# Row halves of the TensorE array for the second rotary product of the attention scores

## The chip, the cores and the metric

The kernel runs on one core of a Trainium2 chip. The metric is the device time of one execution in microseconds (us); the kernel before was run three times, and its median is the number to compare with. The engines are TensorE (PE, with its weight loads shown as PEld), VectorE (DVE), ScalarE (ACT), GpSimd (POOL) and SyncE (SP), which here issues most of the DMA transfers. TensorE works from SBUF into PSUM, which has banks of 512 f32 values in each of 128 partitions.

## What is computed

One layer of an encoder for two sequences of 1024 tokens: a low-rank attention with four heads and a Fourier mixing side by side, an output projection, and a feed-forward part. Of this the attention matters here. Each query and key has a part without position (128 dims, here absorbed into the 128 latent dims of the keys) and a rotary part of 64 dims; the rotary key is shared by the four heads:

```python
q = (rmsnorm(q_lat, g_q_lat) @ w_uq).reshape(b, s, MLA_HEADS, QK_DIM)
q_nope, q_pe = q[..., :NOPE_DIM], q[..., NOPE_DIM:]
q_pe = apply_rope(q_pe, cos[:, None, :], sin[:, None, :])
k_pe = apply_rope(k_pe, cos, sin)
sc = (jnp.einsum('bqhd,bkhd->bhqk', qn_b, k_nope)
      + jnp.einsum('bqhr,bkr->bhqk', qp_b, k_pe)).astype(jnp.float32) * scale
p = jax.nn.softmax(sc, axis=-1).astype(v.dtype)
return jnp.einsum('bhqk,bkhd->bqhd', p, v)
```

## The kernel before

All arithmetic on TensorE that must hold f32 precision is done on split numbers: a value x is written as a high part in f32r (copied by ACT in `split`, line 63) and a low part x minus high (DVE, line 64). A product of two split matrices is three matmuls, high times high, high times low, low times high (`mm3`, lines 79 to 81); low times low is left out.

The kernel goes through stages one after the other: input projections and the first Fourier step, the Fourier step over the tokens with its output, the attention, and the feed-forward part, which is by far the longest and uses a Strassen-like scheme of seven products. Stages share the SBUF: pools of tiles are opened and closed, and a tile that lies over an older one waits until that one's readers are done.

In the attention stage a loop of 64 steps goes over the two sequences s, four blocks b of 256 queries, four heads h, and two halves u of 128 queries. A step issues:
- `scores` (line 1025): ten matmuls of 128 rows by 512 columns into two PSUM banks, five for each bank g of 512 keys. Three of them are the latent part (lines 1033 to 1035, stationary `qa`, the absorbed query, high and low), two the rotary part (lines 1036 and 1037, stationary `qp`). Behind them come the maximum over the keys (DVE, line 1042), the exponential (ACT, line 1047) and the division (DVE, line 1049).
- `flip_p` for the step before: eight transposes of the probabilities on TensorE (line 1061) into PSUM tiles of the tag t (two buffers), each four split by ACT and DVE.
- `values` for a head that is finished (24 matmuls through `mm3`), and a part of the output projection, of the norm and of its transposes for an earlier block (`out_step`).
- for the next block of queries, at the fourth and fifth steps of eight, `rope_q`, which computes the rotary queries, and at the sixth and seventh steps `rope_flip`, which transposes them; and `absorb_q` for the next head.

How the rotary part lies: `rope_q` puts the high part of the 64 rotary dims into columns 0 to 63 of a tile and the low part into columns 64 to 127. `rope_flip` transposes this for four heads (line 720), so in `qp` the rows 0 to 63 are the high part and 64 to 127 the low part of the query; ACT copies it out of PSUM at line 722. The keys stand in `lat[0][:, 1]` (high) and `lat[1][:, 1]` (low), where the 64 rotary dims are held twice, in rows 0 to 63 and again in 64 to 127. One matmul of 128 rows so gives the sum of query high and query low times a key part: line 1036 with the key's high part, line 1037 with its low part.

The order of the instructions on each engine is not just the order of the program: the framework plans it at build time with a cost for every instruction, takes what is ready by its plan in the order of the program, and puts the semaphores. So matmuls of `values` can stand between the transposes of `flip_p`. Each engine then works through its queue in order.

Elsewhere the kernel already uses parts of the array: the modulation vectors at lines 214 and 907 are products with 32 columns of the array each, four next to each other, and line 303 uses two of 64 columns. They hold all 128 rows and are in plain f32, without a split. The transposes of line 374 and the products of lines 79 to 81 that stand around them use the whole array.

Of the kernel before, what the change touches and what calls it, by code (L numbers as in the profile page):

```python
# [13 lines left out]
F32R = mybir.dt.float32r  # L14
# [7 lines left out]
P = 128  # L22
# [3 lines left out]
HEADS = 4  # L26
# [27 lines left out]
def hybrid_encoder_kernel(ctx: ExitStack, tc: tile.TileContext, a: dict):  # L54
    nc = tc.nc
# [3 lines left out]
    def rd(t):  # L59
        return t.bitcast(F32)  # L60
# [5 lines left out]
    def first(early, late):  # L66

        tc.add_manual_dep(late, early.name, mybir.DependencyInfo(mybir.DependencyClass.NoSync, mybir.DependencyReason.DATA),
                          reason="order")
# [91 lines left out]
    with ExitStack() as st:  # L161
        p1b = st.enter_context(ExitStack())
        w2 = p1b.enter_context(tc.tile_pool(name="p1b", bufs=1, side="right", reuse_waits="tile"))
        w = st.enter_context(tc.tile_pool(name="p1", bufs=1, reuse_waits="tile"))
# [501 lines left out]
    S = {}  # L666
# [49 lines left out]
    def rope_flip(s, b, u, bankf):  # L716
        sk = S.pop(("sk", s, b, u))
        pt = bankf("pqt", F32R)
        for h in range(HEADS):
            nc.tensor.transpose(pt[:, h, :], sk[:, h, :], identr)  # L720
        qp = e.tile([P, HEADS, P], F32R, tag="qp", name="qp", bufs=4)
        nc.scalar.copy(qp, rd(pt))
        S["qp", s, b, u] = qp

    def absorb_q(s, b, h, bankf):
        ql = S["q", s, b]
# [38 lines left out]
    with ExitStack() as st:  # L765
        early = st.enter_context(ExitStack())
        wa = early.enter_context(tc.tile_pool(name="p2a", bufs=1, reuse_waits="tile"))
        w = st.enter_context(tc.tile_pool(name="p2", bufs=1, side="right", reuse_waits="tile"))
# [148 lines left out]
        for s in range(2):  # L917
            for t in range(8):
                with tc.issue_after(S["ld"]) if s == 1 and t < 2 else ExitStack():
                    fourier_out(s, abn, (1, 2, 3, 0)[t % 4], t // 4)  # L920
                if s == 1 and t < 4:
                    with tc.issue_after(here["st"]):
                        nc.sync.dma_start(*S["ld2"].pop(0))
                if s == 1 and t == 3:
                    load_q(0, 1)
                    ex = tiny.tile([P, 1], F32, name="ex")
                    nc.vector.memset(ex, 0.0)
                    with tc.issue_after(here["a"]):
                        nc.scalar.activation(ex, ex, AF.Exp)
                    with tc.issue_after(here["ed"]):  # L930
                        for u in range(2):
                            rope_q(0, 0, u, bank2)
                if s == 1 and t == 5:
                    with tc.issue_after(here["ed"]):
                        absorb_q(0, 0, 0, bank2)
                    for u in range(2):
                        rope_flip(0, 0, u, bank2t)
                if s == 0:
                    mod2(t)
                    if t in (4, 6):  # L940
                        c = t // 2 - 2
                        with behind():
                            split(wq_h[:, c, :], wq_l[:, c, :], rd(wq_l[:, c, :]))
# [75 lines left out]
    with ExitStack() as st:  # L1019
        w = st.enter_context(tc.tile_pool(name="p3", bufs=1, side="right", reuse_waits="tile"))  # L1020
# [3 lines left out]

        def scores(s, b, h, u):
            lat = S[s][0]
            qa, qp = S["qa", s, b, h], S["qp", s, b, u]
            us = slice(u * P, u * P + P)
            ps = pp.tile([P, N], F32, tag="s", name="ps_s", bufs=2)
            for g in range(2):  # L1030
                gs = slice(512 * g, 512 * g + 512)
                o = ps[:, gs]
                nc.tensor.matmul(o, qa[0][:, us], lat[0][:, 0, gs], start=True, stop=False)
                nc.tensor.matmul(o, qa[0][:, us], lat[1][:, 0, gs], start=False, stop=False)
                nc.tensor.matmul(o, qa[1][:, us], lat[0][:, 0, gs], start=False, stop=False)
                nc.tensor.matmul(o, qp[:, h, :], lat[0][:, 1, gs], start=False, stop=False)
                nc.tensor.matmul(o, qp[:, h, :], lat[1][:, 1, gs], start=False, stop=True)  # L1037
            mx = tiny.tile([P, 1], F32, name="mx")
            nb = tiny.tile([P, 1], F32, name="nb")
            sm = tiny.tile([P, 1], F32, name="sm")  # L1040
            rr = tiny.tile([P, 1], F32, name="rr")
            nc.vector.tensor_reduce(out=mx, in_=ps, axis=AX.X, op=ALU.max)  # L1042
            ins = nc.vector.tensor_scalar(out=nb, in0=mx, scalar1=-SCALE, scalar2=None, op0=ALU.mult).ins
            if "late" in S:
                first(ins, S.pop("late"))
            p = w.tile([P, N], F32, tag="p", name="p", bufs=3)
            nc.scalar.activation(p, ps, AF.Exp, bias=nb, scale=SCALE, accum_out=sm)
            nc.vector.reciprocal(rr, sm)
            nc.vector.tensor_scalar(out=p, in0=p, scalar1=rr[:, 0:1], scalar2=None, op0=ALU.mult)
            S["p", s, b, h, u] = p  # L1050
            S["rr"] = rr
# [83 lines left out]
        for k in range(nit + 4):  # L1135
# [7 lines left out]
            if k < nit:  # L1143
                s, b, h, u = items[k]
                scores(s, b, h, u)
                nxt = items[k + 8 - k % 8] if k + 8 - k % 8 < nit else None
                i = k % 8
                if nxt is not None:
                    if i == 0 and k > 0:
                        load_q(*nxt[:2])  # L1150
                    if i == 3 and nxt[1] == 0:
                        load_seq(nxt[0], w)
                    if i in (3, 4):
                        rope_q(*nxt[:2], i - 3, gbank)
                    if i in (5, 6):
                        rope_flip(*nxt[:2], i - 5, tbank)
                if u == 1 and k + 1 < nit:
                    absorb_q(*items[k + 1][:3], gbank)
# [16 lines left out]
    with ExitStack() as st:  # L1175
        w = st.enter_context(tc.tile_pool(name="p5", bufs=1, reuse_waits="tile"))
# [620 lines left out]
```

## Time and profile before

| what | value |
|---|---|
| median of three runs | 2069.75 us (2067.46 to 2072.49) |
| the profiled execution's own time | 2068.61 us |
| its span in the profile | 2066.8 us |
| instructions | 28651 |
| granted TensorE clock over the span | 0.995 |
| DMA | 370.36 MB, mean 179 GB/s |

A line of a group in the profile gives the source line, the engine, the operation, output and inputs by the program's names, the array used (rows*columns) and the shape, the count, then the busy time and the mean of one. Matmuls are pipelined: a matmul's own duration overlaps that of the next, so durations add up to more than the time that passed, and the step from one start to the next is what one costs. In a time line a row gives the start and the duration in us; equal neighbours are drawn into one row with their count, and a bracket gives the idle time before and what ended it. "issue" means that nothing in the profile explains the idle time.

### The profile page before, as it was taken

How to read it: one execution, taken by the hardware profiler on the slowest of the kernel's cores; microseconds unless marked ns; L12 is line 12 of the kernel's file. 1: busy time of each engine (PE TensorE's matmuls, PEld its weight loads, DVE VectorE, ACT ScalarE, POOL GpSimd, SP SyncE). 2: the span in 40 equal slices, each digit the busy share in tenths (PEclk: the TensorE clock that was granted, in tenths of full speed). 3: DMA queues.
4: the chain of work that ended last, by engine and by line, in shares of the span. 5: the costliest groups of instructions: out<-in, count | busy, mean ns of one | idle time of the engine just before them, and what ended most of it. 6: DMA issues, size and time to landing. Idle time of an engine off the chain costs nothing.

```text
span 2066.8 us, 28651 instructions
## 1 busy us (share of the span) xinstructions
PE 2018.9 (98%) x9994; PEld 1652.4 (80%) x9994; DVE 1406.0 (68%) x2078; ACT 898.4 (43%) x1753; POOL 841.4 (41%) x1014
## 2 busy tenths in 40 slices
PE   7899999999999999999999999999999999999998
PEld 4688778888888877888888888877788888888876
DVE  4567757766776778777777676778665665667685
ACT  2655535555555564232323355454333323336441
POOL 0555412111313227778778510333554454420142
PEclk9999999999999999999999999999999999999999
DMA  9675784533644375545545587665322222258662
GB/s 389 210 252 169 240 296 149 143 87 88 169 122 134 128 256 188 202 154 194 192 150 208 168 283 253 219 237 176 118 97 102 100 105 102 87 176 280 223 227 98
DMA packets 182685, 370.36 MB, mean 179 GB/s; under 512 B 18412, under 2 KB 57964, under 8 KB 179468
## 3 DMA queue, kind: packets, MB, share of 16 engines
q1 hardware_dynamic: 165196, 315.04, 45.0%
q0 software_dynamic: 17344, 53.49, 8.7%
q8 instruction: 78, 1.28, 0.3%
q14 instruction: 67, 0.55, 0.1%
HBM read 256.46 MB, written 120.39 MB: 182 GB/s over the span
## 4 chain that ended last, share of the span: by engine, by line
PE 55%; DVE 3%; DMA 2%; ACT 1%; POOL 1%; issue 1%; SPq 0%; DVEq 0%; ACTq 0%; POOLq 0%
PE bank L81 18%; PE bank L79 18%; PE bank L80 18%; DVE wl L64 1%; DMA draw<-t_d 1%; ACT wh L63 1%; DVE val L137 1%; DVE val L1599 0%; DMA val<-x_d 0%; DMA X<-hc_d 0%; DVE val L134 0%; DMA rgu<-in_wgu_dram 0%; DMA ga<-ga_d 0%; DMA draw<-s_d 0%; POOL rs_y L105 0%
## 5 line engine op out<-in xcount | busy, mean ns | idle before, releaser
L79 PE MATMUL bank<-H,wh 128*128 128x512 f32 x1232 | 487.6, 396 | 3.8 <-DVE val L137 1.9
L81 PE MATMUL bank<-H,wl 128*128 128x512 f32 x1232 | 488.4, 397 | 0.2 <-DVE wl L64 0.2
L80 PE MATMUL bank<-H,wh 128*128 128x512 f32 x1232 | 484.5, 393 | 0.3 <-DVE H L64 0.3
L79 PEld LDWEIGHTS bank<-H,wh 128*128 128x128 f32 x1232 | 231.3, 188 | 60.0 <-DVE val L137 2.8
L80 PEld LDWEIGHTS bank<-H,wh 128*128 128x128 f32 x1232 | 231.3, 188 | 57.9 <-DVE H L64 0.6
L81 PEld LDWEIGHTS bank<-H,wl 128*128 128x128 f32 x1232 | 231.3, 188 | 57.1 <-DVE wl L64 0.5
L64 DVE TENSOR_TENSOR wl<-draw,wh 128x512 fp32r<-128x512 f32 x286 | 201.9, 739 | 82.6 <-ACT wh L63 79.5
L137 DVE TENSOR_TENSOR val<-bank,val 128x512 f32<-128x512 f32 x200 | 136.6, 689 | 157.1 <-PE bank L81 151.6
L63 ACT CAST wh<-draw 128x512 fp32r<-128x512 f32 x286 | 168.8, 620 | 158.0 <-PE bank L80 91.4
L137 POOL TENSOR_TENSOR val<-val 128x512 f32<-128x512 f32 x58 | 83.5, 1447 | 367.0 <-DVE val L1573 189.2
L80 PE MATMUL bank<-wl,wh 128*128 128x512 f32 x572 | 223.7, 391 | 2.6 <-DVE wl L64 2.6
L63 ACT CAST wh<-rgu 128x512 fp32r<-128x512 f32 x172 | 106.8, 621 | 270.3 <-PE bank L80 210.8
L79 PE MATMUL bank<-wh 128*128 128x512 f32 x572 | 222.6, 389 | 0.0
L81 PE MATMUL bank<-wh,wl 128*128 128x512 f32 x572 | 222.6, 389 | 0.0
L63 ACT CAST wh<-val 128x512 fp32r<-128x512 f32 x133 | 82.3, 621 | 268.7 <-PE bank L80 249.2
L64 DVE TENSOR_TENSOR wl<-val,wh 128x512 fp32r<-128x512 f32 x133 | 133.5, 1005 | 78.1 <-ACT wh L63 77.9
L64 DVE TENSOR_TENSOR wl<-rgu,wh 128x512 fp32r<-128x512 f32 x172 | 164.3, 955 | 5.2 <-ACT wh L63 5.2
L134 POOL TENSOR_TENSOR val<-rgu 128x512 f32<-128x512 f32 x80 | 117.8, 1473 | 101.8 <-DMA rgu<-in_wgu_dram 98.0
L80 PEld LDWEIGHTS bank<-wl,wh 128*128 128x128 f32 x572 | 107.3, 188 | 28.6 <-DVE wl L64 6.4
L79 PEld LDWEIGHTS bank<-wh 128*128 128x128 f32 x572 | 107.4, 188 | 22.4
L81 PEld LDWEIGHTS bank<-wh,wl 128*128 128x128 f32 x572 | 107.4, 188 | 21.9
L1042 DVE TENSOR_REDUCE mx<-ps_s 128x1 f32<-128x1024 f32 x64 | 78.1, 1221 | 61.7 <-PE ps_s L1037 61.4
(356 smaller groups left out, 4113.0 us busy)
## 6 DMA issues: line engine op xcount, KB each, us to landing
rgu<-in_wgu_dram SPq DMA_DIRECT2D x86, 512.0 KB
draw<-s_d SPq DMA_DIRECT2D x143, 256.0 KB
s_d<-val POOLq DMA_DIRECT2D x88, 256.0 KB, 4.1
draw<-t_d SPq DMA_DIRECT2D x88, 256.0 KB
s_d<-val SPq DMA_DIRECT2D x66, 256.0 KB
draw<-in_w_down_dram SPq DMA_DIRECT2D x55, 256.0 KB
wada<-in_w_ada_dram SPq DMA_DIRECT2D x11, 1024.0 KB
xt<-in_x_dram SPq DMA_DIRECT2D x16, 512.0 KB
```

The lines of the kernel that those rows point to most:

```text
L63: here["a"] = nc.scalar.copy(hi, src).ins
L64: here["v"] = nc.vector.tensor_tensor(out=lo, in0=src, in1=rd(hi), op=ALU.subtract).ins
L79: nc.tensor.matmul(out, lh, rh, start=first, stop=False, skip_group_check=cont)
L80: nc.tensor.matmul(out, lh, rl, start=False, stop=False, skip_group_check=cont)
L81: here["t"] = nc.tensor.matmul(out, ll, rh, start=False, stop=last, skip_group_check=cont).ins
L134: return eng.tensor_tensor(out=out, in0=x, in1=y, op=ALU.subtract).ins
L137: eng.tensor_tensor(out=out, in0=x, in1=y, op=ALU.add)
L1042: nc.vector.tensor_reduce(out=mx, in_=ps, axis=AX.X, op=ALU.max)
```

## The change

For all blocks but the very first (which is prepared in the stage before), `rope_flip` makes a second copy `qx` of the high part of the query: ACT reads rows 0 to 63 of the transposed tile and writes them to rows 64 to 127 of `qx`, which has four buffers in the pool of the stage. `scores` no longer treats the two banks one after the other throughout. First come the three latent matmuls for bank 0 and for bank 1, then the product with the key's low part, for bank 0 from rows 0 to 63 of `qp` and of the key, for bank 1 from rows 64 to 127 of `qx` and of the key, so that the two lie in the two row halves of the array, and last the product with the key's high part for both banks in all 128 rows. Query low times key low, which the 128 rows of line 1037 had included, is no longer in the sum. The first eight steps, which have no `qx`, keep 128 rows.

```diff
         qp = e.tile([P, HEADS, P], F32R, tag="qp", name="qp", bufs=4)
         nc.scalar.copy(qp, rd(pt))
-        S["qp", s, b, u] = qp
+        qx = None
+        if (s, b) != (0, 0):
+            qx = w.tile([P, HEADS, P], F32R, tag="qx", name="qx", bufs=4)
+            nc.scalar.copy(qx[64:], rd(pt)[:64])
+        S["qp", s, b, u] = qp, qx
...
-            qa, qp = S["qa", s, b, h], S["qp", s, b, u]
+            qa, (qp, qx) = S["qa", s, b, h], S["qp", s, b, u]
...
             for g in range(2):
                 gs = slice(512 * g, 512 * g + 512)
                 o = ps[:, gs]
                 nc.tensor.matmul(o, qa[0][:, us], lat[0][:, 0, gs], start=True, stop=False)
                 nc.tensor.matmul(o, qa[0][:, us], lat[1][:, 0, gs], start=False, stop=False)
                 nc.tensor.matmul(o, qa[1][:, us], lat[0][:, 0, gs], start=False, stop=False)
-                nc.tensor.matmul(o, qp[:, h, :], lat[0][:, 1, gs], start=False, stop=False)
-                nc.tensor.matmul(o, qp[:, h, :], lat[1][:, 1, gs], start=False, stop=True)
+            for g in range(2):
+                gs = slice(512 * g, 512 * g + 512)
+                kr = slice(0, P) if qx is None else slice(64 * g, 64 * g + 64)
+                nc.tensor.matmul(ps[:, gs], (qx if g == 1 and qx is not None else qp)[kr, h, :], lat[1][kr, 1, gs],
+                                 start=False, stop=False)
+            for g in range(2):
+                gs = slice(512 * g, 512 * g + 512)
+                nc.tensor.matmul(ps[:, gs], qp[:, h, :], lat[0][:, 1, gs], start=False, stop=True)
```

## The prediction

> **What bounds the kernel now.** I read the page first (busy shares, then the chain that ended last), then the table by stage for the attention stage, then the time line of TensorE inside one scores call, and last the places of this kernel where TensorE already works on part of its array. The page's head, its TensorE line and the engines of the chain:
>
> ```profile
> span 2066.8 us, 28651 instructions
> ...
> PE 2018.9 (98%) x9994; PEld 1652.4 (80%) x9994; DVE 1406.0 (68%) x2078; ACT 898.4 (43%) x1753; POOL 841.4 (41%) x1014
> ...
> PE 55%; DVE 3%; DMA 2%; ACT 1%; POOL 1%; issue 1%; SPq 0%; DVEq 0%; ACTq 0%; POOLq 0%
> ```
>
> TensorE is the engine that carries the chain. The stage of the change is the attention stage, from 316 to 735 us; the table by stage gives it as (busy us of PE, PEld, DVE, ACT, POOL, then the granted clock):
>
> ```profile
> 316.00:735.00 419.00, 414.30 (x2595) 364.08 (x2593) 297.17 (x553) 230.25 (x480) 96.92 (x154) 1.00 0.45 124
> ```
>
> TensorE is busy for 414 of 419 us there, at full clock, and ACT for 230. So what one scores call takes on TensorE goes nearly in full into the time. A busy matmul overlaps its neighbours, so the price of one is read from start to start. One half of a scores call on the time line:
>
> ```profile
> 499.16 0.40 PE L1034 MATMUL ps_s<-lat,qa 128*128 128x512 f32 x1
> 499.39 0.40 PE L1035 MATMUL ps_s<-lat,qa 128*128 128x512 f32 x1
> 499.63 0.39 PE L1036 MATMUL ps_s<-lat,qp 128*128 128x512 f32 x1
> 499.85 0.39 PE L1037 MATMUL ps_s<-lat,qp 128*128 128x512 f32 x1
> 500.08 0.40 PE L1033 MATMUL ps_s<-lat,qa 128*128 128x512 f32 x1
> ```
>
> Each starts 0.23 us after the one before (499.16 to 500.08 is 0.92 for four): 0.23 us is the price of a matmul here, and its weight load is hidden.
>
> **The change, part by part.**
>
> (1) The pair. Ten matmuls of a call stay ten, but the two of L1037 now use 64 rows each, rows 0 to 63 for bank 0 and 64 to 127 for bank 1, and stand next to each other. If they run side by side, the second costs only the step between their starts. The first eight of the 64 calls keep the full rows, so 56 change. Does an array cut into parts run side by side in this kernel, and what does it cost to go there and back? No row of before has a row half; the nearest are the column parts of L907 (four of 32 columns) and L303 (two of 64), in plain f32:
>
> ```profile
> 249.56 0.40 PE L81 MATMUL bank<-wm,B 128*128 128x512 f32 x1
> 249.89 0.64 PE L907 MATMUL bank<-wada,scT 128*32 128x512 f32 x4
> ...
> 250.34 0.61 PE L907 MATMUL bank<-wada,scT 128*32 128x512 f32 x4
> 250.89 0.50 PE L79 MATMUL bank<-wm,A 128*128 128x512 f32 x1
> 251.22 0.40 PE L80 MATMUL bank<-wm,A 128*128 128x512 f32 x1
> 251.46 0.40 PE L81 MATMUL bank<-wm,A 128*128 128x512 f32 x1
> ...
> 249.89 0.16 PEld L907 LDWEIGHTS bank<-wada,scT 128*32 128x32 f32 x8 [0.36 <-issue]
> 250.88 0.19 PEld L79 LDWEIGHTS bank<-wm,A 128*128 128x128 f32 x1 [0.84 <-issue]
> 250.99 0.19 PEld L80 LDWEIGHTS bank<-wm,A 128*128 128x128 f32 x1
> ...
> 159.69 0.38 PE L374 MATMUL bank<-ident,xt 128*128 128x128 f32 x2
> 160.00 0.65 PE L303 MATMUL bank<-wada,lw 128*64 128x512 f32 x2
> ...
> 160.48 1.03 PE L303 MATMUL bank<-wada,lw 128*64 128x512 f32 x4
> ...
> 160.91 1.03 PE L303 MATMUL bank<-wada,lw 128*64 128x512 f32 x4
> ```
>
> (A row with x2 or x4 shows the first start of so many.) Four parts take one slot: the four of 249.89 last 0.64 together, and the next four begin 0.45 later. Inside the cut array the pairs of L303 go every 0.43 (160.48 to 160.91), the price of one such f32 matmul. So parts do run side by side. The price of the way there and back stands in the same rows:
> - in: L81 to L907 takes 0.33 where 0.23 is the matmul: 0.10 of empty array. (159.69 is the last but one of transposes 0.11 apart, so the last starts at 159.80, and L303 0.20 later: 0.09 too.)
> - the first load after that is not hidden: for 64 columns the first pair of L303 takes 0.48 instead of 0.43. For the 128 columns of the new pair I take the way out's value, 0.10.
> - out: the last four of L907 to L79 take 0.55, of which 0.45 is their slot: 0.10.
> - the full load after it is not hidden: L79 to L80 takes 0.33 instead of 0.23, 0.10. The load rows say why: L79's load stood idle for 0.84 and began only with its matmul.
>
> Sum of a call: 0.10 + 0.10 + 0.10 + 0.10 for the way there and back, less 0.23 − 0.01 = 0.22 for the matmul that no longer takes a slot: +0.18 us. Times 56: **+10.1 us**. Bounds: −0.22 a call (−12.3 us) if nothing is paid for switching, as below; +0.40 a call (+22.4 us) if the switch is paid and the halves run one after the other. I take the value between, since L907 and L303 show both the gap and the overlap, at every place where they meet full matmuls.
>
> The Trainium skill says so as a rule: "TensorEngine Tiling (Array Packing)", Key Properties, has a change of tiling mode drain the engine, and tiles that work in parallel. The rows above agree with both for columns (0.10 in, 0.10 out, four starts in one slot); no row here shows it for row halves.
>
> Not every narrow matmul pays. These use 2 columns, in f32r like the scores:
>
> ```profile
> 314.56 0.39 PE L80 MATMUL bank<-wm,B 128*128 128x512 f32 x1
> 314.78 0.40 PE L81 MATMUL bank<-wm,B 128*128 128x512 f32 x1
> 315.02 0.40 PE L79 MATMUL bank<-wm,A 128*2 128x512 f32 x1
> 315.25 0.40 PE L80 MATMUL bank<-wm,A 128*2 128x512 f32 x1
> ```
>
> There the steps stay 0.22 to 0.24: size alone costs nothing, the gap belongs to the cut array. These lie at one place and are not run side by side, so they say little for a pair that is.
>
> (2) What of it hides. Some transposes after a scores call wait today for a buffer that ACT or DVE empties (the waits of the weight-load queue between 317 and 740 us, total and times, and one of them):
>
> ```profile
> PEld ppt L1061 <- issue: 4.0, 11, 1.0
> PEld ppt L1061 <- ACT ht L1004: 1.4, 7, 0.2
> PEld ppt L1061 <- ACT qp L722: 1.3, 7, 0.2
> ...
> 422.23 0.39 PE L1037 MATMUL ps_s<-lat,qp 128*128 128x512 f32 x1
> 423.22 0.86 PEld L1061 LDWEIGHTS ppt<-ident,p 128*128 128x128 f32 x8 [0.33 <-issue]
> ```
>
> Where a longer call lies ahead of such a wait, TensorE comes later and waits less. The first two rows are 18 waits, at 0.18 at most 3.2 us; at least nothing. I take **−2.5 us**, near the upper end, because 4.0/11 and 1.4/7 are waits of 0.36 and 0.20, longer than what is added.
>
> (3) The second copy on ACT. It reads 64 of the 128 partitions but the same 512 elements each, so it costs what the first costs, 0.59 us, 14 times (two for each of seven later blocks of queries): 8.3 us of ACT, which has 189 us free in this stage. Behind it on ACT wait the split of the next transposes and, later, the exponential. It also holds the transposes' PSUM buffer longer:
>
> ```profile
> L722 ACT CAST qp<-pqt x16: 587/587/591, 308.8 to 678.1; 128x512 fp32r<-128x512 f32 x16
> ...
> 508.53 0.42 PEld L1061 LDWEIGHTS ppt<-ident,p 128*128 128x128 f32 x4
> 508.77 0.59 ACT L722 CAST qp<-pqt 128x512 fp32r<-128x512 f32 x1 [3.65 <-PE pqt L720]
> 509.25 0.59 ACT L63 CAST pt<-ppt 128x512 fp32r<-128x512 f32 x1
> 509.41 0.42 PEld L1061 LDWEIGHTS ppt<-ident,p 128*128 128x128 f32 x4 [0.18 <-ACT qp L722]
> ```
>
> The transposes of 509.41 already wait 0.18 for the first copy; behind a second one the wait could grow by 0.59. Ends: nothing (the planner puts other ready matmuls ahead, as it did between 508.53 and 509.41) and all of it, 8.3 us. Less than nothing is excluded: a copy more frees nothing sooner. I take **+1.5 us**, near the 1.3 us of today's seven waits.
>
> (4) The order within a call. L1036 now ends the call and both banks close there. The maximum reads both banks, so it starts no earlier or later for that; I cost it at nothing. If another instruction is planned in between the two halves, that call pays +0.40 instead of +0.18.
>
> (5) Four buffers of 2 KB for the copies move the pool of this stage down. Its first loads are queued on SP behind the stores of the stage before, and their first reader comes several steps later; I cost it at nothing. Without that cover a load of weights would come late once, not per call.
>
> Sum: 10.1 − 2.5 + 1.5 = **+9.1 us**. The profiled execution took 2068.61 us, with a span of 2066.8, so 2077.7 for one like it. The median of the three runs shown is 2069.75, 1.1 us above it: 2078.9, rounded to **2079 us**.
>
> **The rivals.**
> - *Faster: no gap for row halves* (the columns keep their full width, as in the rows at 315.02, and rows that are not loaded are simply left out). Then a call saves 0.22, 12.3 us; 2.5 us come back as longer waits of part (2), and the copy takes 1.5: −8.3, **2061 us**. It decides once the way there and back costs under 0.22 a call, about half of the 0.40 that the rows of L907 give. The Trainium skill's "TensorE: Matmul & The Clock Gate", Part 3, has row-packed matmuls start about 4 ns apart and names no gap. For it speaks that f32r with 2 columns pays nothing; against it, that every entry into a really cut array pays. 0.18.
> - *Slower still: gap, but no overlap*, because the two halves' loads or matmuls go one after the other: +0.40 a call, 22.4, less 3.2 hidden, plus 1.5: +20.7, **2090 us**. Against it: the four of L907 and pairs of L303 overlap. For it: the halves share their output columns, which column parts do not. 0.12.
> - *The pair does not do what it says*: half-filled matmuls in the uncut array, no gap and no overlap. Only the copy is left, +1.5: **2071 us**. For it speaks L79 with 2 columns; against it, that an operand at rows 64 to 127 has to name its place in the array. 0.08.
>
> **How the numbers follow.** My forecast has the rest, 0.62. Its own range is 2073 to 2087: 10.1 − 3.2 + 0 = 6.9 at the low end and 10.1 + 8.3 − 2.5 = 15.9 at the high one, with 1.5 us below and above for an order of instructions planned anew and for the runs' own spread. From there the range reaches over the third rival to 2068 and over the second to 2092; left out are the first, 0.18, and a little of the tails. Since 0.2% (4.1 us, 2065.6 to 2073.9) is what measuring this kernel can tell from no change: slower is my forecast and the second rival, 0.74; the same is the third and a remainder of the first, 0.08; faster is 0.18.
>
> **What would show it.** In the changed kernel's time line the two half matmuls start within 0.02 us of each other; the step from the last full matmul to the first half is about 0.33, from the pair to the first full one after it about 0.43 (slot, unhidden load, emptying), and from that to the next 0.33. The weight loads of the first half and of the first full one show idle time before them. Steps of 0.23 throughout mean the third rival; two halves together without longer steps, the first. Waits of the transposes on the query copy grow from 1.3 us if part (3) is larger than I take it; the waits of L1061 shrink if part (2) is right. The prediction is wrong above all if a row half is reached without emptying the array.

## The result and the profile after

The changed kernel took 2077.04 us (median of seven runs, 2073.17 to 2079.54), the kernel before beside it 2068.54 us (2065.57 to 2072.49): a ratio of 1.0039, with a 95% interval of 1.0027 to 1.0051. That is 8.5 us slower by the medians, 8.1 by the ratio (5.6 to 10.5), where 9.1 was forecast.

The page of the changed kernel answers to the one of before: head, TensorE line, engines of the chain.

```profile
span 2077.8 us, 28676 instructions
...
PE 2028.9 (98%) x9994; PEld 1637.7 (79%) x9994; DVE 1402.1 (67%) x2078; ACT 905.5 (44%) x1767; POOL 838.5 (40%) x1014
...
PE 54%; DVE 3%; DMA 2%; issue 1%; POOL 1%; ACT 1%; SPq 0%; DVEq 0%; ACTq 0%; POOLq 0%
```

TensorE has the same 9994 matmuls and is busy for 10 us more; ACT has 14 instructions more, the copies. The place is read from the 64 maxima, one for each step of the attention loop (min, median and max duration in ns, then first and last start in us). First before, then changed:

```profile
L1042 DVE TENSOR_REDUCE mx<-ps_s x64: 1206/1224/1226, 319.2 to 730.8; 128x1 f32<-128x1024 f32 x64
```

```profile
L1052 DVE TENSOR_REDUCE mx<-ps_s x64: 1206/1225/1226, 321.7 to 742.0; 128x1 f32<-128x1024 f32 x64
```

From the first to the last it was 411.6 us and is 420.3: +8.7 us, all in the stage of the change. (The spans differ by 11.0 us because this execution came to the stage 2.5 us later. In the profiled executions of all runs the first maximum starts between 318.2 and 322.0 us; in the run with the copy by DMA, whose code is the same up to there, it starts at 319.0. So this is no part of the change, and the medians are the better measure.) One scores call of the changed kernel in the time line, matmuls and then weight loads:

```profile
505.87 0.40 PE L1039 MATMUL ps_s<-lat,qa 128*128 128x512 f32 x1
506.19 0.50 PE L1043 MATMUL ps_s<-lat,qp 64*128 64x512 f32 x1
506.20 0.50 PE L1043 MATMUL ps_s<-lat,qx 64*128 64x512 f32 x1
506.63 0.73 PE L1047 MATMUL ps_s<-lat,qp 128*128 128x512 f32 x2
...
506.19 0.18 PEld L1043 LDWEIGHTS ps_s<-lat,qp 64*128 64x128 f32 x1 [0.36 <-issue]
506.20 0.18 PEld L1043 LDWEIGHTS ps_s<-lat,qx 64*128 64x128 f32 x1
506.63 0.30 PEld L1047 LDWEIGHTS ps_s<-lat,qp 128*128 128x128 f32 x2 [0.25 <-issue]
```

The halves (64*128) start 0.01 apart, so they do run side by side. The step into them is 0.32 instead of 0.23, the step out of them 0.43, and both times the weight load stood idle before it. Over all 56 calls the steps are, as medians from the starts in the trace:

```
last latent -> first half 327 ns, first half -> second half 3 ns,
pair -> first full one 429 ns, first full one -> second full one 338 ns
```

That is 1097 ns for four steps that took 4 times 232 before (the median step between neighbouring scores matmuls there): +0.169 us a call, times 56 is 9.5 us. The waits of the weight-load queue in this stage (us in total, times, longest) answer to the three rows of before:

```profile
PEld ps_s L1043 <- issue: 20.4, 56, 0.4
PEld ps_s L1047 <- issue: 13.7, 56, 0.2
PEld ppt L1071 <- ACT qx L726: 4.1, 14, 0.3
PEld ppt L1071 <- issue: 2.2, 7, 1.0
```

The first two are the 56 ways in and the 56 ways out. The transposes' waits for the query copy grew from 1.3 us over 7 to 4.1 us over 14. Those called issue shrank from 4.0 to 2.2, and those on ACT's `ht`, 1.4 us, are gone.

### The profile page after: what moved, and what is told of

Same layout as the page of the kernel before. It is cut to its first block, busy times and chain, and to the rows that moved or that the text cites. A ratio compares the mean times of both kernels' runs of the same rounds, so it can differ in the third digit from the quotient of the medians.

```text
span 2077.8 us, 28676 instructions
## 1 busy us (share of the span) xinstructions
PE 2028.9 (98%) x9994; PEld 1637.7 (79%) x9994; DVE 1402.1 (67%) x2078; ACT 905.5 (44%) x1767; POOL 838.5 (40%) x1014
## 4 chain that ended last, share of the span: by engine, by line
PE 54%; DVE 3%; DMA 2%; issue 1%; POOL 1%; ACT 1%; SPq 0%; DVEq 0%; ACTq 0%; POOLq 0%
PE bank L80 18%; PE bank L81 18%; PE bank L79 18%; DVE wl L64 1%; DMA val<-x_d 1%; DVE val L137 1%; DMA draw<-s_d 1%; DMA draw<-t_d 1%; POOL val L137 1%; DVE val L1609 0%; ACT wh L63 0%; DVE val L134 0%; DMA rgu<-in_wgu_dram 0%; POOL rs_y L105 0%; DVE H L64 0%
```

## The experiments

My theory: the price is the way into and out of the cut array, 0.40 us each time, against 0.22 us for a slot saved; the copy and the waits are small. The rivals: the new order costs something by itself; the copy does it; the price hangs on the half matmuls, not on the switch. In the comparisons below a difference in us is the ratio less one, times the median of the kernel before that was run beside it.

**The order alone.** Ten matmuls in 128 rows, in the new order, without `qx`:

```diff
-                kr = slice(0, P) if qx is None else slice(64 * g, 64 * g + 64)
-                nc.tensor.matmul(ps[:, gs], (qx if g == 1 and qx is not None else qp)[kr, h, :], lat[1][kr, 1, gs],
-                                 start=False, stop=False)
+                nc.tensor.matmul(ps[:, gs], qp[:, h, :], lat[1][:, 1, gs], start=False, stop=False)
```

> The order of the changed kernel alone: all ten matmuls of a call in 128 rows, no second copy; low-key products for both banks, then high-key products. Theory (the time is the way into and out of the cut array): no difference from before, within 2 us, and every step in a call 0.23 us. Rival (the new order, closing both banks at the end of the call, costs something by itself): 2 to 9 us slower with no switch at all.

2069.57 us against 2071.85, ratio 0.9993 (0.9984 to 1.0002): no difference, at most 0.4 us slower. The median step between neighbouring scores matmuls is 233 ns, as before. The order is not the cause.

**The copy alone.** The kernel before, with the copy added and not read:

```diff
         nc.scalar.copy(qp, rd(pt))
+        if (s, b) != (0, 0):
+            qx = w.tile([P, HEADS, P], F32R, tag="qx", name="qx", bufs=4)
+            nc.scalar.copy(qx[64:], rd(pt)[:64])
```

> The kernel before with the second copy on ScalarE added and never read, scores as before. Theory: the transposes wait for it at the sixth and seventh of eight steps, 0.3 us more each over 14 steps at most, so 1.5 to 4 us slower. Rival (the copy's 8.3 us of ScalarE come through in full, and the row halves cost nothing): 8 us slower. Rival (hidden altogether): no difference.

2071.93 us against 2071.85, ratio 1.0003 (0.9994 to 1.0012), so between 1.2 us faster and 2.5 slower. Its waits of the weight-load queue in the stage:

```profile
PEld ppt L1064 <- ACT qx L725: 4.1, 14, 0.3
PEld ppt L1064 <- issue: 4.0, 11, 1.0
```

The copy makes 4.1 us of waits by itself, as in the changed kernel, 2.8 more than before; the other waits stay at 4.0 and, on `ht`, at 1.4, since no call is longer. Its 64 maxima go over 414.2 us, 2.6 more than before, but the runs as a whole do not resolve it:

```profile
L1045 DVE TENSOR_REDUCE mx<-ps_s x64: 1207/1225/1226, 320.3 to 734.5; 128x1 f32<-128x1024 f32 x64
```

The full 8.3 us are excluded.

**Both products in one half.** Rows 0 to 63 for both banks, so that nothing can run side by side, without `qx`:

```diff
-                kr = slice(0, P) if qx is None else slice(64 * g, 64 * g + 64)
-                nc.tensor.matmul(ps[:, gs], (qx if g == 1 and qx is not None else qp)[kr, h, :], lat[1][kr, 1, gs],
-                                 start=False, stop=False)
+                kr = slice(0, P) if (s, b) == (0, 0) else slice(0, 64)
+                nc.tensor.matmul(ps[:, gs], qp[kr, h, :], lat[1][kr, 1, gs], start=False, stop=False)
```

> Both low-key products in rows 0 to 63, so that they cannot run side by side; no second copy. Theory: switch paid, slot not saved: 0.40 us a call times 56 is 22.4 us, less about 3 us that hides in waits, so 17 to 22 us slower than before; the two halves start 0.23 us or more apart. Rival (side by side does not matter, the gap comes from the halves' weights): as the changed kernel, 9 us slower.

2086.84 us against 2071.85, ratio 1.0078 (1.0065 to 1.0090): 16 us slower, by the middle just under the expected 17 to 22. The steps of the 56 calls are:

```
last latent -> first half 327 ns, first half -> second half 338 ns,
second half -> first full one 323 ns, first full one -> second full one 337 ns
```

That is 1325 ns instead of 928: 0.397 us a call, 22.2 us, which is the second rival of the prediction worked out on the chip. It also takes the way apart: 0.10 of empty array in (327), 0.11 of unhidden load (338), 0.09 of empty array out (323), 0.11 of unhidden load (337). What was mis-sized is how much hides. Its 64 maxima go over 428.9 us, 17.3 more than before:

```profile
L1047 DVE TENSOR_REDUCE mx<-ps_s x64: 1209/1225/1227, 318.2 to 747.1; 128x1 f32<-128x1024 f32 x64
```

So 4.9 us of the 22.2 do not show, and waits of the weight-load queue have shrunk:

```profile
PEld ps_s L1042 <- issue: 20.5, 56, 0.4
PEld ps_s L1039 <- issue: 20.4, 56, 0.4
PEld ppt L1066 <- issue: 1.8, 3, 1.0
PEld pqt L720 <- DVE pt L64: 1.3, 1, 1.3
```

The transposes' 18 waits of 5.4 us are down to 3 of 1.8, which is 3.6 of the 4.9. Three smaller waits, on `qa`, before `gb` and behind the last matmul of a call, are 1.2 us shorter together and make up nearly all of the rest.

**The halves apart.** As changed, but each half followed at once by the full product of its bank:

```diff
                 nc.tensor.matmul(ps[:, gs], (qx if g == 1 and qx is not None else qp)[kr, h, :], lat[1][kr, 1, gs],
                                  start=False, stop=False)
-            for g in range(2):
-                gs = slice(512 * g, 512 * g + 512)
                 nc.tensor.matmul(ps[:, gs], qp[:, h, :], lat[0][:, 1, gs], start=False, stop=True)
```

> The halves and the second copy as in the changed kernel, but each half followed at once by the full product of its bank, so that the array is cut and restored twice a call and nothing runs side by side. Theory: 2 times 0.40 a call, 0.80 times 56 is 45 us, plus 1.5 to 3 for the copy, less about 3 in waits: 40 to 46 us slower than before. Rival (the gap is paid once per call whatever the order, or by the number of half matmuls): 9 to 22 us slower.

2109.78 us against 2071.85, ratio 1.0186 (1.0172 to 1.0200): 38.5 us slower (35.6 to 41.4), a little less than the 40 to 46 expected. A call:

```profile
508.09 0.40 PE L1039 MATMUL ps_s<-lat,qa 128*128 128x512 f32 x1
508.41 0.50 PE L1043 MATMUL ps_s<-lat,qp 64*128 64x512 f32 x1
508.84 0.50 PE L1045 MATMUL ps_s<-lat,qp 128*128 128x512 f32 x1
509.27 0.50 PE L1043 MATMUL ps_s<-lat,qx 64*128 64x512 f32 x1
509.70 0.50 PE L1045 MATMUL ps_s<-lat,qp 128*128 128x512 f32 x1
510.04 0.28 PE L79 MATMUL gb<-wq_h,ql 128*128 128x256 f32 x1
```

After the first way in (0.32), every change of shape shows a step of 0.43 instead of 0.23, in either direction: 0.10 of empty array for the change itself and 0.10 for the load left open by the one before; the last of these loads is in the step of 0.34 at the end. Against the run with both products in one half it has as many half matmuls, also none side by side, and twice the switches: 0.78 us a call more than before instead of 0.40. So the price is the switch, not the half matmul.

**Two calls for one switch.** The pairs of both query halves of a head stand together, behind the first call's latent products (the second call's product starts its banks):

```diff
+            todo2 = [] if pre is not None else [(ps, qp, qx, False)]
+            if u == 0 and qx is not None:
+                nx = S["ps", s, b, h, 1] = pp.tile([P, N], F32, tag="s", name="ps_s", bufs=2)
+                todo2.append((nx, *S["qp", s, b, 1], True))
+            for pt_, a_, b_, new in todo2:
+                for g in range(2):
...
+                    nc.tensor.matmul(pt_[:, gs], (b_ if g == 1 and b_ is not None else a_)[kr, h, :], lat[1][kr, 1, gs],
+                                     start=new, stop=False, skip_group_check=new)
```

> The pairs of two calls of a head (both halves of 128 queries) next to each other behind the first call's latent products, so that 28 ways into and out of the cut array replace 56. Theory (the price is the way there and back, 0.40 us, and a pair saves 0.22): two calls pay 0.40 and save 0.44, 28 times -0.04 is about -1 us, plus 2.7 us for the copy: within 4 us of before, 6 to 10 us faster than the changed kernel; inside the cut array the second pair starts 0.34 us after the first, the 0.11 of the unhidden first load included. Rival (the price hangs on the number of half matmuls or of row halves used, not on entering and leaving): as the changed kernel, 8 us slower than before. Rival (holding the second call's PSUM banks earlier makes TensorE wait for the exponential): 5 us or more slower, with waits on that.

2074.80 us against 2071.26, ratio 1.0016 (1.0008 to 1.0025): 3.3 us slower, within 4 us of before as expected, but against the changed kernel's 8.1 us only about 5 better, not 6 to 10. Where the pairs stayed together the call is as forecast (rows of the time line), and the way in is paid once for two pairs:

```profile
482.19 0.49 PE L1049 MATMUL ps_s<-lat,qp 64*128 64x512 f32 x1
482.19 0.50 PE L1049 MATMUL ps_s<-lat,qx 64*128 64x512 f32 x1
482.52 0.39 PE L1049 MATMUL ps_s<-lat,qp 64*128 64x512 f32 x1
482.53 0.39 PE L1049 MATMUL ps_s<-lat,qx 64*128 64x512 f32 x1
482.86 0.74 PE L1053 MATMUL ps_s<-lat,qp 128*128 128x512 f32 x2
```

The waits of its weight-load queue on the half matmuls:

```profile
PEld ps_s L1049 <- issue: 12.8, 35, 0.4
PEld ps_s L1049 <- ACT p L1063: 1.5, 4, 0.4
```

But there are more ways in than 28. The first row counts 35, one more is among the four waits of the second row, and the starts in the trace give 36: 20 for two pairs, and 16 for one pair alone. The planner had torn the pairs of eight heads, in seven of them with matmuls of `values` between. Waits for the second call's banks (on the exponential `p`) are 1.5 us.

**The copy by DMA.** The changed kernel, with the copy taken from ACT:

```diff
-            nc.scalar.copy(qx[64:], rd(pt)[:64])
+            nc.sync.dma_start(rd(qx)[64:], rd(qp)[:64])
```

> The changed kernel with its second copy made by a DMA on the SP queue out of the first copy, instead of by ScalarE. Theory: the waits of the transposes go back from 4.1 to 1.3 us, so 2 to 3 us faster than the changed kernel, 5 to 7 us slower than before. Rival (the copy costs nothing): as the changed kernel, 8 us slower than before.

2077.31 us against 2071.26, ratio 1.0028 (1.0017 to 1.0039): 5.8 us slower, in the expected 5 to 7; the interval, 3.5 to 8.1, just holds the rival's 8. The trace is clearer: the waits on the query copy are back at 1.3 us over 7 times, and the 64 maxima go over 418.0 us, 2.3 less than in the changed kernel.

**Both edits together.**

> Both edits together: two pairs for one way into and out of the cut array, and the second copy by DMA. Theory: -1 us from the pairs and nothing from the copy: within 2 us of before, on either side; nothing to win beyond that. Rival: 3 us or more faster than before, if waits of the stage shrink further; or 4 us or more slower, if the second call's banks are held too early.

2073.42 us against 2071.26, ratio 1.0012 (1.0002 to 1.0021): 2.5 us slower, a little outside the 2 us expected; the interval is 0.4 to 4.2. It too has 36 ways in.

**The pairs tied.** As the version with both edits, with the half matmuls tied to each other and behind the latent products, and the second call's pair put first, so that all 28 pairs of pairs hold:

```diff
-                todo2.append((nx, *S["qp", s, b, 1], True))
+                todo2.insert(0, (nx, *S["qp", s, b, 1], True))
...
+                    with tc.issue_after(last) if last is not None else ExitStack():
+                        last = nc.tensor.matmul(pt_[:, gs], (b_ if g == 1 and b_ is not None else a_)[kr, h, :], lat[1][kr, 1, gs],
+                                                start=new, stop=False, skip_group_check=new).ins
```

> As the version with two pairs at a time and the second copy by DMA, with the four half matmuls tied to each other and behind the first call's latent products, so that no pair is torn: 28 ways into the cut array instead of 35. Theory (each way there and back is 0.40 us): 7 times 0.40 is 2.8 us less, so 1 us faster than before, within 2 us of it on either side. Rival (what is left of that version's 2.4 us comes from waits for the second call's PSUM banks): still 2 to 4 us slower than before, with the waits on the exponential grown.

2069.59 us against 2070.63, ratio 0.9995 (0.9986 to 1.0005): no difference from before, between 2.9 us faster and 1.0 slower. The trace has 28 ways in, eight fewer than the version with both edits (the expectation counted seven), which is 3.2 us at 0.40; the runs put 3.5 us between the two versions, with intervals as wide as that. With two pairs for one switch 0.40 is paid and twice 0.23 saved. The six steps of a call are 1327 ns instead of 1392, 0.07 us less, or 1.8 us over 28 calls, which these runs cannot tell from nothing. The trace also has a single wait that belongs to no switch: in the first head that is tied, the second call's half waits for its copy by DMA.

```profile
PEld ps_s L1050 <- DMA qx<-qp: 3.2, 1, 3.2
```

The version with both edits, which takes the first call's pair first, has no such wait. In the trace the wait takes back what the eight switches give: the 64 maxima go over 414.4 us, against 414.6 with both edits. What two pairs for one switch would win without this wait was not tried; in these runs they break even, and nothing is won on the kernel before.

## Why the prediction was right

The time, 2077.04 us, lies in the range and 2 us under the number; 1.2 of these 2 us are the kernel before, whose median was 2068.54 beside it and not 2069.75. By its parts:

- (1) The pair: +0.18 us a call was forecast from column parts in plain f32, 0.169 was measured for row halves in f32r. All four terms held: 0.10 in, 0.11, 0.09 out, 0.11, and 3 ns between the halves. The step from the pair to the full ones was forecast as 0.43 and is 0.429. The rule of the Trainium skill, "TensorEngine Tiling (Array Packing)", Key Properties, that a change of tiling mode drains the engine, agrees with the trace for rows as well (0.10 of empty array in, 0.09 out); the price is the trace's.
- (2) What hides: −2.5 us was taken, at most −3.2. The two kinds of wait went from 5.4 to 2.2 us, so it was the upper end, −3.2. With a larger price more hid (4.9 us where both products shared a half), so that bound holds only for a call longer by 0.18.
- (3) The copy: +1.5 us was taken, between 0 and 8.3. The waits on it grew by 2.8 us, here and with the copy alone. This term was mis-sized, by 1.3 us: instead of seven waits of 0.18 there are fourteen of 0.3. Of the 8.1 us that the fourteen copies take (579 ns each) 2.8 came through.
- (4) The order: nothing was forecast and nothing was found, by the run with the order alone.
- (5) The pool that moved: not tried alone; it is in the run with the copy alone, which shows no difference.

The sum by these readings is 9.5 − 3.2 + 2.8 = 9.1 us; the stage shows 8.7. The 0.4 between them is less than what single other waits moved (the query transposes' wait on DVE went from 1.3 to 0.7 us). That the sum comes out at the forecast 9.1 is luck: the terms are off by −0.6, −0.7 and +1.3, and these cancel. The sign, the price of the switch and the overlap are not luck.

One bound of the prediction does not follow from its working: the low end of the forecast's own range is given as 2073, but 2069.75 + 6.9 − 1.5 is 2075.1 (2074.0 from the profiled execution). The time lies above either.

The rivals: no gap for row halves fell with the step of 0.32 into them. The Trainium skill's "TensorE: Matmul & The Clock Gate", Part 3, is right that packed matmuls start some 4 ns apart (3 ns here), but that counts from a cut array already entered. Gap without overlap is the run with both products in one half, 16 us. Halves in the uncut array fell with the 3 ns.

## What to carry to other kernels

Packing two half-height matmuls into one slot of TensorE pays only if the array stays cut long enough: here the way in and out cost 0.40 us and a pair of 512 columns saved 0.23, so one pair for each switch lost and two broke even. Before such a change, look in the same trace for places where the array is already cut, and read the steps into and out of them from start to start. Check also that the planner keeps the packed matmuls together, since every torn pair pays the whole switch again.

## What the runs showed that I had not expected

A first load of 64 rows after the switch costs as much as one of 128: the unhidden part is 0.11 us both ways (steps of 338 and 337 ns where both products share a half), and the loads themselves last 183 ns against 188 (the lines of the changed kernel, min, median and max in ns):

```profile
L1039 PEld LDWEIGHTS ps_s<-lat,qa x128: 186/188/192, 319.4 to 740.3; 128*128 128x128 f32 x128
L1043 PEld LDWEIGHTS ps_s<-lat,qx x56: 182/183/183, 358.5 to 740.8; 64*128 64x128 f32 x56
```

Half the rows make the load no cheaper. Inside the cut array loads are hidden again: with two pairs for one switch the second pair's starts are 0.33 after the first's, which is a slot and the first pair's own load, and the step out of the second pair is 0.32 where the one out of a lone pair is 0.43.

The planner tears pairs that stand together in the program: it takes what is ready by its plan, and matmuls of `values` came between. In seven of the eight torn heads one pair stood ahead of the first call's last latent products. The tied version holds all 28 with both pairs behind the latent products and the halves behind each other; whether the second tie alone would do was not tried.
